# Norms of keys and queries from matmuls with ones, one chain of roots per head, and ScalarE Sqrt in the last stage

## The chip, the cores and the metric

The kernel runs on one core of a Trainium2 chip. The metric is the device time of one execution in microseconds (us); the times shown are medians of several executions. The engines are named as in the profile: PE (TensorE, matmuls), PEld (its weight loads), DVE (VectorE), ACT (ScalarE), POOL (GpSimd) and SP (SyncE, which issues nearly all the DMAs here).

## The reference

One layer of a hybrid encoder on a sequence of 2048 tokens and 1024 channels. Cut to what matters:

```python
h = rms_norm(x, norm_w) * (1.0 + scale) + shift          # scale, shift, gate from c
proj = h @ w_in                                          # u_a, z_a, qkv, z_b, beta, alpha
y = s5_direction(u, ..., False) + s5_direction(u, ..., True) + s5_d * u
y_a = glu(gelu(y)) * jax.nn.silu(z_a)                    # branch A: state space

qkv = jax.nn.silu(centred_depthwise_conv(qkv, conv_w))   # 5 taps, per channel
q = l2_normalize(to_heads(q)) * (DN_HEAD_DIM ** -0.5)    # 4 heads of 128
k = l2_normalize(to_heads(k))
o = gated_delta_chunked(q, k, v, g_f, beta_f) + flip(gated_delta_chunked(flip(q), ...))
o = o * lax.rsqrt(jnp.mean(o * o, axis=-1) + NORM_EPS) * dn_norm_w
y_b = o * jax.nn.silu(z_b)                               # branch B: gated delta rule

x = x + gate * (jnp.concatenate([y_a, y_b]) @ w_out)
out = rms_norm(x, final_norm_w)

def l2_normalize(t):
    return t * lax.rsqrt(jnp.sum(t * t, axis=-1, keepdims=True) + NORM_EPS)
```

The two places that the change touches are `l2_normalize` of K and Q, and the two root-mean-square norms at the end, that of `o` (128 channels of a head) and that of the output row (1024 channels).

## The kernel before

The stages follow each other: the modulation and `h` with the first columns of the projection (to about 195 us), the projection with the convolutions of K, Q and V beside the preparation of the state-space branch (to about 800), the inverses of the delta rule's chunks, and from about 1200 us the last stage, in which the scan over chunks, the output projection and the final norm run together.

**Ticks.** The projection works in ticks. `job(i, evac)` takes one block of 128 columns of `w_in`; for each of its four blocks of 512 tokens, `gemm` runs 24 matmuls of 128x512 (three products of 16-bit halves, tiles `hhi`, `hlo`, `wh`, `wl`) into a PSUM bank of the pool `gm`, `evac` takes the bank out, and `tick()` runs what is due. `later(n, fn)` puts `fn` n ticks on. The order in which the functions are called is the order on each engine's queue. The columns come in the order: u, part of z_a, beta and alpha, four heads of K, four of Q, then V in turn with the rest of z_a and z_b. Each head's block takes its steps one tick apart: `tap` (ACT, first tap, L1014), `conv` (DVE, four operations on 128x512, L1021), `gated` (ACT Silu, L1027), `turn` (PE, four transposes to PSUM, L1037; ACT, four Squares with a sum each, L1046), `norm` (DVE: for K the root `rk` and the product `kt`, L1056, L113 to L120, L1059; for Q only `iq2`, L1053), and for K `back` (PE, four transposes of `kt`, L1066; ACT copy, L1068).

`rsqrt` is a chain of 11 DVE operations: two on integers for a first guess (L113, L115) and three rounds of three (L118 to L120).

**The state-space branch** runs as a generator, `side`, of which `tick` takes one step. In its tables, `s5_tables`, POOL forms 12 products of 128x512 per group (`cpw`, `bpw`, `tmp`, helper line L502), PE transposes `bpw` into the pool `sq`, ACT copies it to `bpt` (L832, one buffer for two copies per group) and SP stores it to `cb_d`; other matmuls give `lk`, which ACT copies (L852) and POOL adds to.

**PSUM.** The pools are `gm` with 2 banks, `pt` with 3 and `sq` with 2. Transposes of K, Q and V, the column maxima (`w_max`: a matmul of `w` with `ones` for the scale of the next weights, DVE L135 to L139) and later stages share `pt`. The next weights' low half is `wl` (DVE, L215).

**The last stage** follows order strings written by hand, one letter for each step of a generator:

```python
S9 = "qqqqsssssssqsssqlttltststqstrrsrrtssssssltrltrr"
in_order(order, s=seq(s), l=ahead_of(s + 1), a=part(ag, NA[s]),
         p=product(prev) if prev is not None else iter(()), q=prepare(s - 1), r=product(s - 1),
         t=prepare(NCH - s))
```

`seq(s)` is a step of the scan (tiles `z`, `vn`, `S`, `tq`), `prepare(ch)` norms a chunk of `o` (`rs`, then POOL's `on`, L1718, PE's transposes, L1722, DVE's `yb`, L1724, ACT's `oyh`), and `product(ch)` makes 128 rows of the output (`r`, norm `r1`, store). There are 16 of each.

Of the kernel before, what the change touches and what calls it, by code (L numbers as in the profile page):

```python
# [40 lines left out]
def block(ctx, tc, x, c, ada_w, ada_b, norm_w, w_in, conv_w,  # L41
# [66 lines left out]
    def rsqrt(pool, dst, src, tag):  # L108

        shp = list(src.shape)  # L110
        y = pool.tile(shp, F32, tag=tag + "y", name=tag + "y")
# [1 line left out]
        V.tensor_scalar(out=t.bitcast(I32), in0=src.bitcast(I32), scalar1=1, scalar2=None,  # L113
                        op0=ALU.arith_shift_right)
        V.tensor_scalar(out=y.bitcast(I32), in0=t.bitcast(I32), scalar1=-1.0,  # L115
                        scalar2=float(0x5F3759DF), op0=ALU.mult, op1=ALU.add)
        for it in range(3):
            V.tensor_tensor(out=t, in0=y, in1=y, op=ALU.mult)  # L118
# [1 line left out]
            V.scalar_tensor_tensor(out=(dst if it == 2 else y), in0=t, scalar=1.5, in1=y,  # L120
                                   op0=ALU.add, op1=ALU.mult)
# [678 lines left out]
    def s5_tables(gb, st5, sc_, bt):  # L800
# [26 lines left out]
        for i in range(2):  # L827
            ps = bank("sq", (128, GB, 128))
            for j in range(GB):
                nc.tensor.transpose(ps[:, j], bpw[i][:, j].rearrange("p t q -> p (t q)"), ident)  # L830
# [1 line left out]
            A.activation(out=bpt, in_=ps, func=AF.Copy)  # L832
# [19 lines left out]
        A.activation(out=l0, in_=lk[0][:, 0:SN], func=AF.Copy)  # L852
# [145 lines left out]
    def conv_job(i, kind, h):  # L998
# [26 lines left out]
        def gated(tb):  # L1025
            cv = cvs[tb]
            A.activation(out=cv, in_=cv, func=AF.Silu)  # L1027
# [4 lines left out]
        def turn(tb):
# [5 lines left out]
            if kind == 2:  # L1038
# [3 lines left out]
                return  # L1042
            ss = sp.tile([128, 4], F32, tag="ss", name="ss")
            for j in range(4):
                jk = sp.tile([128, 128], BF16, tag="jk", name="jk")
                A.activation(out=jk, in_=ps[:, j * 128:(j + 1) * 128], func=AF.Square,  # L1046
                             accum_out=ss[:, j:j + 1])
# [2 lines left out]
        def norm(ps, ss, c4):  # L1050
            if kind == 0:

                V.tensor_scalar(out=iq2[:, c4, h], in0=ss, scalar1=EPS, scalar2=128.0, op0=ALU.add, op1=ALU.mult)  # L1053
                return
            rk = sp.tile([128, 4], F32, tag="rk", name="rk")
            V.tensor_scalar(out=ss, in0=ss, scalar1=EPS, scalar2=None, op0=ALU.add)  # L1056
            rsqrt(sp, rk, ss, "rk")
            kt = tp.tile([128, 4, 128], F32, tag="kt", name="kt")
            V.tensor_tensor(out=kt, in0=ps.rearrange("p (c d) -> p c d", d=128), in1=bc(rk, 128), op=ALU.mult)  # L1059
# [636 lines left out]
    def prepare(ch):  # L1696
# [16 lines left out]
        V.scalar_tensor_tensor(out=sq, in0=sq, scalar=1.0 / 128, in1=t, op0=ALU.mult, op1=ALU.add)  # L1713
# [4 lines left out]
        P.tensor_tensor(out=on, in0=o_, in1=bc(rs, 128), op=ALU.mult)  # L1718
# [15 lines left out]
    def product(ch):  # L1734
        yh, yl, xt = bs_.pop(ch)
        r = ot.tile([128, D], F32, tag="r", name="r", bufs=2)
        s2 = ot.tile([128, 2], F32, tag="s2", name="s2", bufs=2)
# [9 lines left out]
        jk = ot.tile([128, D], BF16, tag="jkr", name="jkr")  # L1747
        for n in range(2):
            ns = slice(n * 512, (n + 1) * 512)
            A.activation(out=jk[:, ns], in_=r[:, ns], func=AF.Square, accum_out=s2[:, n:n + 1])  # L1750
# [2 lines left out]
        V.tensor_tensor(out=s1, in0=s2[:, 0:1], in1=s2[:, 1:2], op=ALU.add)
# [4 lines left out]
        V.scalar_tensor_tensor(out=r, in0=r, scalar=r1, in1=fnw, op0=ALU.mult, op1=ALU.mult)
# [80 lines left out]
```

## Time and profile before

| what | value |
|---|---|
| median of 3 runs | 1452.25 us (1451.58 to 1455.87) |
| profiled execution | 1450.6 us |
| its span, first to last instruction | 1448.9 us |
| mean granted clock of PE | 0.947 |
| busy: PE, DVE, ACT, POOL | 1288.1, 1143.8, 683.0, 728.6 us |
| DMA, mean over the span | 142 GB/s |

The shares are averages over stages with different limits. Where two engines are both busy for most of a stage, the windows of the profile tell which of them waits. The granted clock is that of the windows' own rows: 1.00 is full speed.

### The profile page before, as it was taken

To read this page: it belongs to the slowest core of one execution; us is meant where nothing else is said; L and a number is where in the kernel's file an instruction comes from. 1 tells how busy PE (TensorE), PEld (TensorE's weight loads), DVE (VectorE), ACT (ScalarE), POOL (GpSimd) and SP (SyncE) were. 2 spreads that over 40 slices of the span, in tenths; PEclk is the share of its full clock that TensorE was granted. 3 is DMA by queue.
4 is the path that set the end of the run, shared out by engine and by line. 5 is a ranking of instruction groups with operands and counts; after the bars stand their busy time and mean duration, and the time that the engine had idled before them with its cause. 6 is when DMAs were issued, how large, how long until landed. Compare 5 with 4: busy or idle time off the path is not lost.

```text
span 1448.9 us, 26795 instructions
## 1 busy us (share of the span) xinstructions
PE 1288.1 (89%) x9744; PEld 890.1 (61%) x9744; DVE 1143.8 (79%) x2483; ACT 683.0 (47%) x1571; POOL 728.6 (50%) x680
## 2 busy tenths in 40 slices
PE   2879897888879988999999799999999988899996
PEld 2435343444444444555455578999998776788884
DVE  4645588999988899999984667888887467998875
ACT  4445222445546545353446566777666322323322
POOL 3223123763553377878760666556652234554443
PEclk9889998988989999999999899999999999899998
DMA  9454433224326533443424523544435487486532
GB/s 314 152 132 138 104 68 93 62 70 142 105 88 166 155 98 99 132 123 96 139 76 147 156 72 110 169 140 140 125 118 191 152 298 271 165 300 209 189 118 79
DMA packets 255284, 206.46 MB, mean 142 GB/s; under 512 B 88496, under 2 KB 206256, under 8 KB 255152
## 3 DMA queue, kind: packets, MB, share of 16 engines
q1 hardware_dynamic: 255152, 204.75, 45.6%
q8 instruction: 77, 1.26, 0.4%
q14 instruction: 55, 0.45, 0.1%
HBM read 133.38 MB, written 73.33 MB: 143 GB/s over the span
## 4 chain that ended last, share of the span: by engine, by line
PE 50%; DVE 32%; DMA 5%; issue 4%; POOL 3%; ACT 2%; SPq 1%; POOLq 0%; DVEq 0%; ACTq 0%
PE gm L33 27%; PE sq L33 13%; PE pt L33 8%; DVE cv L1021 6%; DVE w L502 3%; DVE xs L930 2%; DVE rkt L119 1%; DVE wl L215 1%; DVE rkt L118 1%; DMA y<-ya_d 1%; DVE tm L502 1%; DVE r L1744 1%; DMA cb_d<-bpt 1%; DVE rky L120 1%; PE pt L1037 1%
## 5 line engine op out<-in xcount | busy, mean ns | idle before, releaser
L33 PE MATMUL gm<-hhi,wh 128*128 128x512 f16 (+1 forms) x784 | 297.5, 396 | 13.0 <-ACT wh L213 6.9
L33 PE MATMUL gm<-hhi,wl 128*128 128x512 f16 (+1 forms) x784 | 295.5, 392 | 13.4 <-DVE wl L215 13.4
L33 PE MATMUL gm<-hlo,wh 128*128 128x512 f16 (+1 forms) x784 | 296.5, 394 | 0.0
L33 PEld LDWEIGHTS <-wh 128*128 128x128 f16 (+1 forms) x1664 | 154.3, 100 | 202.7 <-issue 31.2
L1021 DVE SCALAR_TENSOR_TENSOR cv<-raw,cw,cv 128x512 f32<-128x512 f32 x192 | 185.7, 970 | 9.2 <-ACT cv L1014 3.2
L33 PEld LDWEIGHTS <-wl 128*128 128x128 f16 (+1 forms) x832 | 80.2, 100 | 114.6 <-DVE wl L215 18.0
L502 POOL TENSOR_TENSOR w<-w,w 128x512 f32<-128x512 f32 x32 | 50.1, 1574 | 73.3 <-DVE w L502 73.3
L33 PE MATMUL gm<-yh,gwh 128*128 128x256 f32 x256 | 80.0, 313 | 6.3 <-ACT yh L770 5.3
L1006 ACT ACTIVATE raw<-gm,w 128x512 f32<-128x512 f32 x48 | 33.1, 690 | 110.4 <-PE gm L33 110.4
L1745 POOL TENSOR_TENSOR r<-r,xt 128x512 f32<-128x512 f32 x32 | 45.7, 1429 | 69.0 <-DVE r L1744 33.7
L33 PE MATMUL gm<-yl,gwh 128*128 128x256 f32 x256 | 73.4, 287 | 0.7 <-POOL yl L771 0.7
L33 PE MATMUL gm<-yh,gwl 128*128 128x256 f32 x256 | 72.5, 283 | 0.0
L1413 ACT ACTIVATE Y<-pt 128x512 f16<-128x512 f32 x96 | 57.9, 603 | 25.6 <-PE pt L33 24.8
L33 PE MATMUL sq<-S,kq 128*128 128x128 f32 x480 | 65.4, 291 | 0.0
L930 DVE TENSOR_TENSOR_SCAN xs<-c,w 128x255 f32<-128x255 f32 x64 | 63.5, 1050 | 2.2 <-POOL w L502 2.2
L33 PEld LDWEIGHTS sq<-S,kq 128*128 128x128 f32 x480 | 63.0, 205 | 2.0
L1392 DVE CAST_PREDICATED pb<-msk,pt 128x512 f16<-128x512 int8 x80 | 56.7, 711 | 6.5 <-PE pt L33 5.3
L33 PE MATMUL pt<-Y,nh 128*128 128x64 f16 (+1 forms) x896 | 56.3, 198 | 4.6 <-DVE Y L1400 4.2
L312 POOL TENSOR_SCALAR hhi<-hf 128x512 f16<-128x512 f32 x32 | 30.0, 957 | 54.7 <-ACT hf L310 47.4
L1414 ACT ACTIVATE YT<-pt 128x512 f16<-128x512 f32 x96 | 57.3, 597 | 0.0
L994 ACT ACTIVATE z<-gm,w 128x512 f32<-128x512 f32 x32 | 22.0, 687 | 74.1 <-PE gm L33 43.2
L1665 POOL TENSOR_TENSOR ra<-ra,xh 128x512 f32<-128x512 f32 x14 | 18.8, 1346 | 75.4 <-DVE ra L1664 44.7
(455 smaller groups left out, 3627.7 us busy)
## 6 DMA issues: line engine op xcount, KB each, us to landing
xt<-in_x_dram SPq DMA_DIRECT2D x25, 512.0 KB
ws<-in_w_in_dram SPq DMA_DIRECT2D x24, 512.0 KB
aw<-in_ada_w_dram SPq DMA_DIRECT2D x24, 512.0 KB
kq<-kT_d SPq DMA_DIRECT2D x32, 256.0 KB
kq<-qT_d SPq DMA_DIRECT2D x32, 256.0 KB
kt<-kt_d SPq DMA_DIRECT2D x32, 256.0 KB
vt<-vt_d SPq DMA_DIRECT2D x32, 256.0 KB
out_dram<-r SPq DMA_DIRECT2D x16, 512.0 KB
```

Of the source, the lines that this page charges most:

```text
L33: nc.tensor.matmul(out, lhsT, rhs, start=start, stop=stop)
L312: P.tensor_scalar(out=hhi[:, k, sl], in0=hf, scalar1=1.0, scalar2=1.0, op0=ALU.mult, op1=ALU.mult)
L502: (e or V).tensor_tensor(out=o, in0=a, in1=b, op=op)
L930: V.tensor_tensor_scan(out=o, data0=m1, data1=v, initial=0.0, op0=ALU.mult, op1=ALU.add)
L994: A.activation(out=z, in_=ps, func=AF.Silu, scale=iv)
L1006: A.activation(out=raw[:, 2 + tb * 512:2 + (tb + 1) * 512], in_=ps, func=AF.Copy, scale=iv)
L1021: V.scalar_tensor_tensor(out=cv, in0=raw[:, o + j:o + j + 512], scalar=cw[:, i12, j:j + 1], in1=cv, op0=ALU.mult, op1=ALU.add)
L1392: V.copy_predicated(out=cols(PB[d][li], b, d), mask=mb, data=pp.rearrange("p t (n b) -> p t n b", b=b))
L1413: A.activation(out=cols(Y[d], b, d), in_=pa.rearrange("p t (n b) -> p t n b", b=b), func=AF.Copy)
L1414: A.activation(out=cols(YT[d], b, 1 - d), in_=pb.rearrange("p t (n b) -> p t n b", b=b), func=AF.Copy)
L1665: P.tensor_tensor(out=r_, in0=r_, in1=x_, op=ALU.add)
L1745: P.tensor_tensor(out=r[:, ns], in0=r[:, ns], in1=xt[:, ns], op=ALU.add)
```

## The change

1. **K and Q.** ACT squares the convolved block in one operation of 128x512 (`sq`, before the transposes), and `total` sums it over channels with four PE matmuls against a column of ones into a `pt` bank. `taken` (DVE) brings the four columns to SBUF: into `ss` for K, into `iq2` for Q. Q isn't transposed any more. K has one `rsqrt` for a head, on 16 columns, after its fourth block; then its four blocks are transposed, one a tick. Functions that are due in the same tick are sorted by a rank.
2. **Tables.** `bpt` has a buffer for each of its two copies, and a `yield` stands between ACT's copies of `lk` and POOL's additions and the store of `lk_d`. Some buffers move: `raw` has two instead of three, `cv` nine instead of five, `kt` three instead of two; `qh` shares the buffer of `q`; scratch of the beta and alpha columns shares that of `sq`.
3. **Last stage.** The root is ACT Sqrt followed, after a `yield`, by `root_fix` on DVE: a reciprocal and one round of three operations. In `product`, one Square over 1024 replaces two over 512 and the addition of their sums; in `prepare`, an operation with `iq2` goes, since `iq2` now holds the factor.

```diff
+    def root_fix(pool, y, src, tag):
+        t = pool.tile(list(src.shape), F32, tag=tag + "t", name=tag + "t")
+        V.reciprocal(out=y, in_=y)
+        V.tensor_tensor(out=t, in0=y, in1=y, op=ALU.mult)
+        V.scalar_tensor_tensor(out=t, in0=t, scalar=-0.5, in1=src, op0=ALU.mult, op1=ALU.mult)
+        V.scalar_tensor_tensor(out=y, in0=t, scalar=1.5, in1=y, op0=ALU.add, op1=ALU.mult)
...
-    rp = p1.enter_context(pool("rp", 3))
+    rp = p1.enter_context(pool("rp", 2))
...
-            bpt = bt.tile([128, GB, 128], F32, tag="bpt", name="bpt")
+            bpt = sc_.tile([128, GB, 128], F32, tag=f"tp{1 + i}", name="bpt", bufs=1)
...
         A.activation(out=lkf[:, W:], in_=lk[0][:, SN:W], func=AF.Copy)
+        yield
         TT(l0, l0, dd[:, gb], ALU.add, P)
...
-        q = mp.tile([128, 2, R // 2], F32, tag="qh", name="qh", bufs=1)
+        q = mp.tile([128, 2, R], F32, tag="q", name="qh", bufs=1)[:, :, 0:R // 2]
...
-        for e in [e for e in late if e[0] <= clock[0]]:
+        for e in sorted((e for e in late if e[0] <= clock[0]), key=lambda e: e[2]):
...
-            later(1, lambda: turn(tb))
+            if kind == 2:
+                later(1, lambda: turn(tb))
+                return
+            sq = tp.tile([128, 512], F32, tag="sq", name="sq")
+            A.activation(out=sq, in_=cv, func=AF.Square)
+            later(1, lambda: total(tb, sq), 2)
+
+        def total(tb, sq):
+            ps = bank("pt")
+            for j in range(4):
+                mm(nc, ps[:, j:j + 1], sq[:, j * 128:(j + 1) * 128], ones[:, 0:1])
+            later(1, lambda: taken(tb, ps), 1)
+
+        def taken(tb, ps):
+            c4 = slice(tb * 4, tb * 4 + 4)
+            if kind == 0:
+                V.tensor_scalar(out=iq2[:, c4, h], in0=ps[:, 0:4], scalar1=EPS, scalar2=128.0 * EPS,
+                                op0=ALU.add, op1=ALU.mult)
+                cvs.pop(tb)
+                return
+            V.tensor_scalar(out=ss[:, c4], in0=ps[:, 0:4], scalar1=EPS, scalar2=None, op0=ALU.add)
+            if tb == NB - 1:
+                rsqrt(sp, rk, ss, "rk")
+                for n in range(NB):
+                    later(1 + n, lambda n=n: turn(n), 2)
...
-            ss = sp.tile([128, 4], F32, tag="ss", name="ss")
-            for j in range(4):
-                jk = sp.tile([128, 128], BF16, tag="jk", name="jk")
-                A.activation(out=jk, in_=ps[:, j * 128:(j + 1) * 128], func=AF.Square,
-                             accum_out=ss[:, j:j + 1])
-            later(1, lambda: norm(ps, ss, c4))
...
+            later(1, lambda: norm(ps, c4), 1)
...
-            later(2, lambda: back(kt, c4))
+            later(2, lambda: back(kt, c4), 1.5)
...
-        t = ot.tile([128, H], F32, tag="sqt", name="sqt")
-        V.tensor_scalar(out=t, in0=iq2[:, ch, :], scalar1=EPS, scalar2=None, op0=ALU.mult)
-        V.scalar_tensor_tensor(out=sq, in0=sq, scalar=1.0 / 128, in1=t, op0=ALU.mult, op1=ALU.add)
+        V.scalar_tensor_tensor(out=sq, in0=sq, scalar=1.0 / 128, in1=iq2[:, ch, :], op0=ALU.mult, op1=ALU.add)
         rs = ot.tile([128, H], F32, tag="rs", name="rs")
-        rsqrt(ot, rs, sq, "ro")
-        yield
+        A.activation(out=rs, in_=sq, func=AF.Sqrt)
+        yield
+        root_fix(ot, rs, sq, "ro")
...
-        for n in range(2):
-            ns = slice(n * 512, (n + 1) * 512)
-            A.activation(out=jk[:, ns], in_=r[:, ns], func=AF.Square, accum_out=s2[:, n:n + 1])
-        yield
-        V.tensor_tensor(out=s1, in0=s2[:, 0:1], in1=s2[:, 1:2], op=ALU.add)
+        A.activation(out=jk, in_=r, func=AF.Square, accum_out=s1)
+        yield
         V.tensor_scalar(out=s1, in0=s1, scalar1=1.0 / D, scalar2=EPS, op0=ALU.mult, op1=ALU.add)
-        rsqrt(ot, r1, s1, "rf")
-        yield
+        A.activation(out=r1, in_=s1, func=AF.Sqrt)
+        yield
+        root_fix(ot, r1, s1, "rf")
```

**Where the instructions stand.** PE in the projection, at the end of a tick in which a K block is turned and another turned back (`gm` are the last matmuls of the tick, `sq<-ident,bpw` the tables' transposes); before:

```order
L33 MATMUL gm<-hhi,wl 128x512
L1066 MATMUL pt<-ident,kt 128x128 x4
L1037 MATMUL pt<-ident,cv 128x128 x4
L830 MATMUL sq<-ident,bpw_2882 128x128 x4
L830 MATMUL sq<-ident,bpw_2883 128x128 x4
L33 LDWEIGHTS wh
```

and a tick of the same kind after:

```order
L33 MATMUL gm<-hhi,wl 128x512
L1092 MATMUL pt<-ident,kt 128x128 x4
L1075 MATMUL pt<-ident,cv 128x128 x4
L33 MATMUL pt<-ones,sq 128x1 x4
L838 MATMUL sq<-ident,bpw_3568 128x128 x4
L838 MATMUL sq<-ident,bpw_3569 128x128 x4
L33 LDWEIGHTS wh
```

A third group stands on the `pt` banks in one tick, the sums of a later block.

DVE in the same part of the program (`cv` are the convolution's steps, `kt` the normed K); before, with a chain for each block:

```order
L1021 SCALAR_TENSOR_TENSOR cv<-raw,cw,cv 128x512 x8
L1056 TENSOR_SCALAR ss<-ss 128x4
L113 TENSOR_SCALAR rkt<-ss 128x4
L115 TENSOR_SCALAR rky<-rkt 128x4
L118 TENSOR_TENSOR rkt<-rky 128x4
L119 SCALAR_TENSOR_TENSOR rkt<-rkt,ss 128x4
L120 SCALAR_TENSOR_TENSOR rky<-rkt,rky 128x4
L118 TENSOR_TENSOR rkt<-rky 128x4
```

and after, between two of the chains:

```order
L1032 SCALAR_TENSOR_TENSOR cv<-raw,cw,cv 128x512 x4
L1063 TENSOR_SCALAR kss<-pt 128x4
L1085 TENSOR_TENSOR kt<-pt,rk 128x512
L223 SCALAR_TENSOR_TENSOR wl<-ws,w_3686,wh 128x1024
L1032 SCALAR_TENSOR_TENSOR cv<-raw,cw,cv 128x512 x4
L1085 TENSOR_TENSOR kt<-pt,rk 128x512
L1063 TENSOR_SCALAR kss<-pt 128x4
```

The chain is gone from between the convolution and `kt`; `kss`, which reads a `pt` bank, and `kt` follow the convolution.

ACT near the end of the last stage (`jk` and `jkr` are the Squares, `oyh` the copy of `yb`); before:

```order
L1709 ACTIVATE jk,sq<-o 128x128 x4
L1640 ACTIVATE ayh<-y_17088 128x512
L1709 ACTIVATE jk,sq<-o 128x128 x4
L1750 ACTIVATE jkr,s_17034<-r 128x512 x2
L1727 ACTIVATE oyh<-yb 128x512 x2
```

and after, with the roots `rs` and `r_16602`:

```order
L1736 ACTIVATE jk,sq<-o 128x128 x4
L1740 ACTIVATE rs<-sq 128x4
L1774 ACTIVATE jkr,s_16601<-r 128x1024
L1753 ACTIVATE oyh<-yb 128x512
L1777 ACTIVATE r_16602<-s_16601 128x1
L1753 ACTIVATE oyh<-yb 128x512
```

The two kinds of root are new on this engine, the first right behind its Squares, the second here behind a copy that waits for DVE's `yb`. In all the program has 33 ACT table loads, where it had 32.

More of the change, by code (lines that the diff above doesn't have):

```diff
@@ L962, in block, with later @@
     clock = [0]
-    def later(n, fn):
-        late.append((clock[0] + n, fn))
+    def later(n, fn, rank=0):
+        late.append((clock[0] + n, fn, rank))
     def tick():
         clock[0] += 1
-        for e in [e for e in late if e[0] <= clock[0]]:
+        for e in sorted((e for e in late if e[0] <= clock[0]), key=lambda e: e[2]):
             late.remove(e)
@@ L1003, in conv_job @@
         cvs = {}
+        if kind == 1:
+            ss, rk = [sp.tile([128, NCH], F32, tag=t, name=t, bufs=2) for t in ("kss", "rk")]
         def evac(tb, ps, iv):
@@ L1012, in tap @@
         def tap(tb):
-            cv = cvs[tb] = tp.tile([128, 512], F32, tag="cv", name="cv", bufs=5)
+            cv = cvs[tb] = tp.tile([128, 512], F32, tag="cv", name="cv", bufs=9)
             A.activation(out=cv, in_=raw[:, tb * 512:tb * 512 + 512], func=AF.Copy, scale=cw[:, i12, 0:1])
@@ L1042, in turn, with norm @@
                 return
-            ss = sp.tile([128, 4], F32, tag="ss", name="ss")
-            for j in range(4):
-                jk = sp.tile([128, 128], BF16, tag="jk", name="jk")
-                A.activation(out=jk, in_=ps[:, j * 128:(j + 1) * 128], func=AF.Square,
-                             accum_out=ss[:, j:j + 1])
-            later(1, lambda: norm(ps, ss, c4))
[L1050 to L1059, printed above, removed]
+            later(1, lambda: norm(ps, c4), 1)
+        def norm(ps, c4):
+            kt = tp.tile([128, 4, 128], F32, tag="kt", name="kt", bufs=3)
+            V.tensor_tensor(out=kt, in0=ps.rearrange("p (c d) -> p c d", d=128), in1=bc(rk[:, c4], 128), op=ALU.mult)
             nc.sync.dma_start(out=kt_d[:, c4, h, :], in_=kt)
-            later(2, lambda: back(kt, c4))
+            later(2, lambda: back(kt, c4), 1.5)
         def back(kt, c4):
@@ L1113, in ab_parts @@
     def ab_parts(av):
-        t = lambda n: tp.tile([128, 2, NCH, H], F32, tag=n, name=n, bufs=1)
         al = av[1]
-        ab_, e, s, s2, w_ = t("abs"), t("e"), t("s"), t("s2"), t("w_")
+        room = [tp.tile([128, 4, 2, NCH, H], F32, tag="sq", name="room") for _ in range(2)]
+        ab_, e, s, s2, w_ = [room[n // 4][:, n % 4] for n in range(5)]
         dnr = tp.tile([128, 4, H], F32, tag="dnr", name="dnr", bufs=1)
@@ L1736, in product @@
         r = ot.tile([128, D], F32, tag="r", name="r", bufs=2)
-        s2 = ot.tile([128, 2], F32, tag="s2", name="s2", bufs=2)
         for n in range(2):
@@ L1747, in product @@
         jk = ot.tile([128, D], BF16, tag="jkr", name="jkr")
-        for n in range(2):
-            ns = slice(n * 512, (n + 1) * 512)
-            A.activation(out=jk[:, ns], in_=r[:, ns], func=AF.Square, accum_out=s2[:, n:n + 1])
+        s1, r1 = [ot.tile([128, 1], F32, tag=t, name=t, bufs=2) for t in ("s1", "r1")]
+        A.activation(out=jk, in_=r, func=AF.Square, accum_out=s1)
         yield
-        s1 = ot.tile([128, 1], F32, tag="s1", name="s1", bufs=2)
-        V.tensor_tensor(out=s1, in0=s2[:, 0:1], in1=s2[:, 1:2], op=ALU.add)
         V.tensor_scalar(out=s1, in0=s1, scalar1=1.0 / D, scalar2=EPS, op0=ALU.mult, op1=ALU.add)
-        r1 = ot.tile([128, 1], F32, tag="r1", name="r1", bufs=2)
-        rsqrt(ot, r1, s1, "rf")
+        A.activation(out=r1, in_=s1, func=AF.Sqrt)
         yield
+        root_fix(ot, r1, s1, "rf")
         V.scalar_tensor_tensor(out=r, in0=r, scalar=r1, in1=fnw, op0=ALU.mult, op1=ALU.mult)
```

## The prediction

> **What bounds the kernel now.** I read the page's busy shares first, then the busy time by stage, then the chain and the groups by line in the two stages that the diff touches, and the timeline where one piece had to be priced.
>
> ```profile
> PE 1288.1 (89%) x9744; PEld 890.1 (61%) x9744; DVE 1143.8 (79%) x2483; ACT 683.0 (47%) x1571; POOL 728.6 (50%) x680
> ```
>
> PE is the fullest engine, but that is an average. The blocks of K and Q go through the convolution from about 252 to 506 us. The next view splits most of that time (window, length, busy us of PE, PEld, DVE, ACT and POOL, granted clock, DMA share, GB/s):
>
> ```profile
> 260.00:300.00 40.00, 34.40 (x224) 16.86 (x221) 38.85 (x59) 15.81 (x45) 33.06 (x26) 0.96 0.23 73
> 300.00:340.00 40.00, 32.68 (x184) 17.23 (x184) 37.48 (x85) 20.29 (x68) 19.98 (x20) 0.87 0.34 99
> 340.00:380.00 40.00, 29.40 (x163) 14.19 (x161) 37.92 (x66) 16.64 (x60) 24.45 (x23) 0.86 0.30 89
> 380.00:420.00 40.00, 30.22 (x196) 16.63 (x197) 35.92 (x91) 18.09 (x61) 16.33 (x15) 0.80 0.43 129
> 420.00:440.00 20.00, 19.71 (x137) 10.88 (x136) 17.39 (x38) 9.94 (x34) 7.60 (x8) 1.00 0.29 86
> 440.00:480.00 40.00, 38.39 (x197) 19.81 (x196) 32.66 (x59) 27.51 (x97) 12.21 (x14) 1.00 0.68 175
> sum 220.00, PE 184.81 PEld 95.59 DVE 200.22 ACT 108.27 POOL 113.63; mean PE 30.80 PEld 15.93 DVE 33.37 ACT 18.05 POOL 18.94
> ```
>
> From 260 to 420 DVE is busy for 90 to 97% of the time while PE waits. PE is idle for 220 - 184.81 = 35.2 us, and it is also slowed: busy time times (1 - clock) is 1.4 + 4.2 + 4.1 + 6.0 = 15.7 us. So there are 51 us of room here, nearly all before 440; after it PE is full. What holds DVE is one chain of roots after another. This is the timeline of one (start, duration), DVE's and then POOL's rows of the same moment:
>
> ```profile
> 311.69 0.98 DVE L113 TENSOR_SCALAR rkt<-ss 128x4 int32<-128x4 int32 x1
> 312.70 0.17 DVE L115 TENSOR_SCALAR rky<-rkt 128x4 int32<-128x4 int32 x1
> 312.90 1.11 DVE L118 TENSOR_TENSOR rkt<-rky 128x4 f32<-128x4 f32 x1
> ...
> 319.64 1.11 DVE L120 SCALAR_TENSOR_TENSOR rk<-rkt,rky 128x4 f32<-128x4 f32 x1
> ```
>
> ```profile
> 311.59 1.05 POOL L502 TENSOR_TENSOR tmp<-pwci,cr 128x512 f32<-128x512 f32 x1
> 312.72 1.27 POOL L502 TENSOR_TENSOR cpw<-cpw,tmp 128x512 f32<-128x512 f32 x1
> ```
>
> Eleven operations on 4 numbers per partition take 9.1 us (311.69 to 320.75), because each wide product on POOL holds up the small DVE operation beside it: 0.98 to 1.11 us instead of 0.17.
>
> The last stage, 1200 to 1449, is another case:
>
> ```profile
> 1200.00:1300.00 100.00, 85.41 (x503) 74.46 (x502) 86.63 (x262) 33.17 (x125) 53.08 (x43) 0.93 0.68 238
> 1300.00:1400.00 100.00, 97.46 (x545) 82.58 (x544) 81.46 (x264) 31.18 (x110) 47.44 (x38) 1.00 0.56 192
> ```
>
> PE has 14.6 us of idle time and 85.41 x 0.07 = 6.0 us of lost clock in the first 100 us, and next to nothing in the second.
>
> **The change, part by part: K and Q.** Their costs, by line from 195 to 800 us (the first row is all DVE work that touches the chains' scratch tile, 16 chains of 11; the last two are the wait lines of ACT and PE):
>
> ```profile
> 195.00:800.00 605.00, 61.39 (x176) 0.94 0.37 109
> L1056 DVE TENSOR_SCALAR ss<-ss 128x4 f32<-128x4 f32 x16 | 5.4, 337 | 0.8 <-ACT jk L1046 0.8
> L1046 ACT ACTIVATE jk<-pt 128x128 bf16<-128x128 f32 x128 | 33.6, 287 | 2.8 <-PE pt L1037 2.8
> L1046 ACT ACTIVATION_READ_ACCUMULATOR jk<-pt 128x1 f32 x128 | 28.0, 220 | 0.0
> L1027 ACT ACTIVATE cv<-cv 128x512 f32<-128x512 f32 x48 | 30.7, 640 | 1.2 <-DVE cv L1021 1.2
> ACT bpt L832 <- DMA cb_d<-bpt: 62.5, 8, 14.7
> PE gm L33 <- DVE wl L215: 13.4, 5, 5.6
> ```
>
> - DVE: a chain costs 61.39/16 = 3.84 us. Four stay of 16, now on 16 columns, which I price alike since the row is time of issue and waiting: -46 us. The 32 `taken` of 0.34 us (row L1056) make 11 us, against 5.4 of `ss` and about as much of Q's, so they cancel. DVE's 200.2 us in the window become about 154.
> - ACT: 128 Squares with their reads go, 61.6 us; 32 Squares of 128x512 come, at the Silu's 0.64 us 20.5. ACT gains 41 us and was not the bound.
> - PE pays. The timeline prices four matmuls with `ones` and four transposes:
>
> ```profile
> 63.63 0.36 PE L33 MATMUL pt<-ones,aw 128*128 128x1 f32 x2
> 63.85 0.36 PE L33 MATMUL pt<-ones,acc 128*128 128x1 f32 x2
> 306.25 0.60 PE L1066 MATMUL pt<-ident,kt 128*128 128x128 f32 x4
> 306.69 0.60 PE L1037 MATMUL pt<-ident,cv 128*128 128x128 f32 x4
> ```
>
>   Starts lie 0.22 us apart, so a block's four sums take 0.9 us and its four transposes 0.44. K keeps its transposes: 16 x 0.9 = 14.3 us. Q loses them: 16 x 0.46 = 7.3. PE gets 21.6 us more, of which 19.8 fall in the window.
> - The room in the window becomes 51 - 20 = 31 us. Not all is had. The next column block's weights (`wl`, 13.4 us of PE's waits) come behind DVE's queue: with DVE a quarter shorter I take half, -6.7. Second, in 13 ticks `back`, `turn` and `total` now use all three `pt` banks, where a K tick used two; PE then waits in the same tick for DVE's `taken` and `norm`, which stand behind four convolution steps. No row shows this wait. The nearest is the idle time ahead of the same transposes, in the last row below: 11.9 us over 48 blocks, 0.25 us each. I take that in each of 32 ticks, since `taken` is new in all, -8.0. Bounds: none, and 1.5 us a tick, the one piece in the row before it, which ended on neither a root nor a `bpt` copy.
> - `bpt`, with two buffers: ACT's 62.5 us of waiting for a store goes. What of it reached PE is in the room already, so nothing is added. The `yield` lets POOL compute the next products instead of waiting for ACT's copies; POOL's 12 products stay, `lk_d` is stored a tick later, behind one tick's other transfers on SP, which issues as many as before. `qh` in `q`'s buffer: both are POOL's, in order. `raw` with two buffers instead of three: a head's last convolution comes three ticks after its last block, and the buffer is wanted again after four, a tick of slack. These I count as nothing; if the cover goes, SP's `kt_d` store, which waits for `kt`, holds `cb_d` behind it, as in the 4.23 us piece of the chain.
>
> ```profile
> 381.27 4.23 DMA cb_d<-bpt
> 444.42 0.66 PE L1037 MATMUL pt<-ident,cv 128*128 128x128 f32 x4 [1.50 <-ACT cv L1027]
> L1037 PE MATMUL pt<-ident,cv 128*128 128x128 f32 x192 | 30.8, 285 | 11.9 <-ACT kk L1068 5.7 <-DVE kt L1059 4.2 <-ACT cv L1027 1.5
> ```
>
> Sum for this stage: 31 - 6.7 - 8.0 - 1.8 (Q's additions after 480) = **14.5 us less**. Bounds: 31 less, and 25 more where the new wait is 1.5 us a tick (32 x 1.5 = 48, against 31 - 6.7 - 1.8 = 22.5 of room).
>
> The row says 46 us less on DVE. A rule would give less: the Trainium skill, "SBUF — State Buffer", section "SBUF: two separate sides", says that DVE (with two SBUF inputs or in a fast mode) and GpSimd take turns on a shared port pair, each for a whole instruction. Then POOL's products only move on to hold up the convolutions, and a chain is worth its own time, 11 x 0.17 = 1.9 us: 12 chains are 22 us. The alternation above agrees; with 22 the stage could gain no more than about that, with 46 up to the 31.
>
> **The last stage.** Rows from 1200 on (first all DVE work on the scratch tile of `rs`, then that of `r1`; 16 chains each), and two prices for ACT from elsewhere:
>
> ```profile
> 1200.00:1449.00 249.00, 39.22 (x176) 0.96 0.54 188
> 1200.00:1449.00 249.00, 35.60 (x176) 0.96 0.54 188
> L1713 DVE SCALAR_TENSOR_TENSOR sq<-sq,sqt 128x4 f32<-128x4 f32 x16 | 9.2, 575 | 2.4 <-ACT jk L1709 1.0
> L118 DVE TENSOR_TENSOR rot<-roy 128x4 f32<-128x4 f32 x48 | 11.0, 229 | 1.6
> L1722 PE MATMUL sq<-ident,on 128*128 128x128 f32 x64 | 11.1, 301 | 14.6 <-POOL on L1718 14.6
> L852 ACT ACTIVATE l<-sq 128x16 f32<-128x16 f32 x8 | 1.8, 219 | 0.0
> L954 ACT ACT_TABLE_LOAD x13 | 16.7, 1283 | 0.2
> ACT oyh L1727 <- DVE yb L1724: 40.4, 9, 8.2
> ```
>
> - Removed: 39.2 + 35.6 us of chains. Added: 32 x 4 operations at L118's 0.229, 29 us (the reciprocal too, which no row shows on so few numbers). DVE gets 46 us back in a stage where it was busy for four fifths. ACT adds 32 Sqrts at 0.22 (7 us) and one more table load in the program, 1.3 us.
> - PE's waits here are for `on`, 14.6 us, and POOL's `on` waits for `rs`. The root was 39.2/16 = 2.5 us; it becomes 0.22 + 4 x 0.23 = 1.1 and two handoffs. But `root_fix` now stands a step later, and the Sqrt stands in ACT's queue, behind copies that wait for others (`oyh`: 40.4/9 = 4.5 us a time). I take half of waits and lost clock, (14.6 + 6.0)/2 = 10.3. Bounds: all of it, -21; three Sqrts behind a waiting `oyh`, +13.
> - The end, where nothing covers:
>
> ```profile
> 1441.31 0.16 DVE L1753 TENSOR_TENSOR s<-s 128x1 f32<-128x1 f32 x1 [1.90 <-ACT jkr L1750]
> 1443.89 1.28 DVE L1758 SCALAR_TENSOR_TENSOR r<-r,r,fnw 128x1024 f32<-128x1024 f32 x1
> ```
>
>   From 1441.31 to 1443.89 are 2.6 us. They become a step of 0.2, a Sqrt of 0.22, four steps of 0.2 and two handoffs of about 0.1: 1.4. The Square over 1024 instead of the second 512 adds some 0.5 (three quarters of the Silu's 0.64): -0.7.
>
> Sum: **11 us less**. Together 1450.6 - 14.5 - 11 = 1425.1 for a profiled execution. The one before stands 1.65 under the median of 1452.25, so 1427.
>
> **Rivals.**
> A. *The PE work and the third bank eat the convolution stage's gain.* Were the new wait 0.7 us a tick instead of 0.25 (32 x 0.7 = 22.5), nothing is left there: 1452 - 11 = 1441. For it: `taken` stands behind four convolution steps. Against it: the steps begin at the tick's start, and 24 matmuls hide them.
> B. *Slower.* The same wait, larger: at 1.05 us a tick the stage has lost the last stage's 11 as well (32 x 1.05 = 33.5) and the sign turns; at the bound of 1.5 it is 25 - 11 more: 1466. For it: POOL's products can hold up each of the four steps ahead. Against it: a wait of that length stands once in the 48 blocks, and only 13 of the 32 ticks need all three banks.
> C. *Full gain.* Both stages reach their bounds, 31 and 21 less: 1400. Half the weights' waits and all waits for `on` would have to go, and DVE and POOL hold each other up still; half way there is 1413.
> D. *The Sqrt reloads tables.* Were a load put ahead of each of 32 Sqrts and one behind it, each root would come 2 x 1.283 = 2.6 us later, less the 1.4 (2.5 - 1.1) that it gains: 16 x 1.2 = 19 us more ahead of `on`, and 1452 - 14.5 + 19 = 1457. The built program has one load more, not 64. The Trainium skill, "ScalarE: Activation LUTs", section "Table sets: the hidden batching unit", has sqrt in a set of its own and tells to batch by set; only Copy and Square stand beside Sqrt here, and no run yet shows them together.
>
> **How the numbers follow.** Forecast 1427 (1416 to 1437): 0.58. A: 0.18. C: 0.13. B: 0.06. D: 0.02. Nothing measurable: 0.03, from between A and B. What lies within 0.3% (4.4 us) can't be told from no change here. A counts as faster but for 0.02: faster 0.87, same 0.05, slower 0.08. The range 1407 to 1446 takes in the forecast, A, and C to half way, and leaves out B, D and the rest of C.
>
> **What would show it.** Right: in the K ticks DVE well under 90%, granted clock over 0.95 from 300 to 420, PE idle from 260 to 480 down from 35 to about 15; no wait of ACT for `cb_d`; PE's wait for `on` about halved and one more table load. Wrong: PE's waits for `taken` or `norm` at `total` and `turn` beyond 0.7 us a tick, or ACT's Sqrt held up behind `oyh` with `on` later than before.

## The result, and the profile after

The changed kernel takes 1428.3 us (median of 4 runs, 1426.4 to 1430.0) against 1454.1 before: a ratio of 0.9829, with a 95% interval of 0.9813 to 0.9845. The forecast was 1427. The sum came out, but not term by term: tried by itself, the convolution stage gave less than forecast and the last stage more. (The pool `sq` has three PSUM banks, not the two that the part on the kernel gives; no step above used that number.)

The profiled execution has a span of 1427.1 us at a mean clock of 0.952. The busy shares of its page:

```profile
PE 1297.3 (91%) x9936; PEld 907.2 (64%) x9936; DVE 1057.0 (74%) x2095; ACT 672.9 (47%) x1348; POOL 733.2 (51%) x680
```

The windows of the convolution stage, as they were shown of before:

```profile
260.00:300.00 40.00, 33.87 (x225) 17.32 (x223) 35.78 (x86) 17.24 (x43) 25.03 (x23) 0.91 0.24 73
300.00:340.00 40.00, 33.99 (x210) 19.53 (x209) 33.38 (x45) 17.25 (x38) 25.62 (x23) 0.91 0.19 53
340.00:380.00 40.00, 36.67 (x250) 21.20 (x249) 34.44 (x45) 18.21 (x36) 28.32 (x23) 0.91 0.39 116
380.00:420.00 40.00, 36.81 (x230) 21.88 (x229) 28.23 (x49) 19.37 (x43) 23.75 (x20) 0.91 0.33 96
420.00:440.00 20.00, 20.00 (x144) 11.68 (x143) 13.97 (x31) 9.21 (x19) 9.20 (x14) 1.00 0.72 196
440.00:480.00 40.00, 39.87 (x228) 23.05 (x227) 24.23 (x49) 21.63 (x37) 0.98 (x1) 1.00 0.83 214
sum 220.00, PE 201.21 PEld 114.67 DVE 170.04 ACT 102.91 POOL 112.90; mean PE 33.54 PEld 19.11 DVE 28.34 ACT 17.15 POOL 18.82
```

PE's idle time fell from 35.2 to 18.8 us, but the clock did not recover: 0.91 in four windows, 12.7 us lost where 15.7 were. Two thirds of what PE still waits for is the release of a PSUM bank, and it waited for such banks before, too. These are the longest of PE's waits from 260 to 480 (total, times, longest) in the kernel before:

```profile
PE gm L33 <- DVE wl L215: 10.5, 3, 5.6
PE pt L1066 <- DVE w L135: 5.9, 1, 5.9
PE pt L1037 <- ACT kk L1068: 5.7, 3, 4.3
PE pt L33 <- DVE kt L1059: 4.6, 1, 4.6
PE pt L1037 <- DVE kt L1059: 4.2, 2, 3.9
```

`kk`, `kt` and `w` are what empties the `pt` banks, so some 21 us of PE's waits were for these banks already. After the change the whole list is this, 12.5 us for `pt`; below it stands the longest wait in the timeline, DVE's rows first:

```profile
PE pt L1075 <- DVE kss L1063: 6.4, 2, 6.0
PE gm L33 <- DVE wl L223: 6.1, 1, 6.1
PE pt L33 <- DVE raw L1011: 3.0, 1, 3.0
PE pt L1075 <- DVE kt L1085: 1.9, 1, 1.9
PE pt L1092 <- DVE kt L1085: 1.2, 1, 1.2
```

```profile
326.75 0.24 DVE L120 SCALAR_TENSOR_TENSOR rk<-rkt,rky 128x16 f32<-128x16 f32 x1
326.91 3.10 DVE L1032 SCALAR_TENSOR_TENSOR cv<-raw,cw,cv 128x512 f32<-128x512 f32 x4
329.93 0.15 DVE L1063 TENSOR_SCALAR kss<-pt 128x4 f32<-128x4 f32 x1
...
330.14 1.11 PE L1075 MATMUL pt<-ident,cv 128*128 128x128 f32 x4 [6.01 <-DVE kss L1063]
```

DVE has a chain of roots and then four convolution steps ahead of a `kss` of 0.15 us, and until `kss` has read its bank PE can't turn the next block.

In the last stage, 100-us windows 25 us earlier than those shown of before (the first `on` comes 7.5 us earlier and the last `r` 20.3, so the places match only roughly; in a window from 1192.5, where the shift of the first `on` would put it, PE is busy for 95.0 us instead of 94.4):

```profile
1175.00:1275.00 100.00, 94.44 (x591) 82.40 (x591) 70.01 (x180) 37.07 (x130) 59.90 (x49) 0.98 0.81 281
1275.00:1375.00 100.00, 93.13 (x520) 80.49 (x519) 59.67 (x154) 31.67 (x112) 44.03 (x36) 0.97 0.57 198
```

The first gained 9 us of PE time and most of its clock; DVE fell from 87% to 70%. The second lost 4 us: it has 6.9 us of idle time, all of it one wait for `on`, which the timeline explains (engines mixed, in order of time):

```profile
1310.29 0.63 ACT L1667 ACTIVATE ayh<-y 128x512 fp32r<-128x512 f32 x1 [8.18 <-DMA y<-ya_d]
1310.95 0.69 DVE L1671 TENSOR_TENSOR ayl<-y,ayh 128x512 fp32r<-128x512 f32 x1 [5.30 <-ACT ayh L1667]
1311.56 0.17 DVE L126 RECIPROCAL rs<-rs 128x4 f32<-128x4 f32 x1
...
1312.16 0.16 DVE L129 SCALAR_TENSOR_TENSOR rs<-rot,rs 128x4 f32<-128x4 f32 x1
1312.49 1.04 POOL L1744 TENSOR_TENSOR on<-o,rs 128x512 f32<-128x512 f32 x1 [8.45 <-DMA of<-o_d]
1313.58 1.12 PE L1748 MATMUL sq<-ident,on 128*128 128x128 f32 x4 [6.87 <-POOL on L1744]
```

ACT's `ayh` waits for the load of `y`, DVE's `ayl` waits for `ayh`, and `root_fix` stands behind `ayl`. POOL's wait is put down to the load of `of`, but POOL starts 0.17 us after `rs` is done (1312.16 + 0.16), so I read `rs` as what let it go.

### The profile page after: what moved, and what is told of

It reads as the page before. It is cut to its first block, busy times and chain, and to the rows that moved or that the text cites. A ratio compares the mean times of both kernels' runs of the same rounds, so it can differ in the third digit from the quotient of the medians.

```text
span 1427.1 us, 26499 instructions
## 1 busy us (share of the span) xinstructions
PE 1297.3 (91%) x9936; PEld 907.2 (64%) x9936; DVE 1057.0 (74%) x2095; ACT 672.9 (47%) x1348; POOL 733.2 (51%) x680
## 3 DMA queue, kind: packets, MB, share of 16 engines
q8 instruction: 78, 1.28, 0.4%
## 4 chain that ended last, share of the span: by engine, by line
PE 64%; DVE 21%; DMA 4%; issue 3%; ACT 3%; POOL 1%; SPq 1%; DVEq 0%; ACTq 0%; POOLq 0%
PE gm L33 36%; PE sq L33 15%; PE pt L33 12%; DVE cv L1032 6%; DVE w L510 2%; DMA y<-ya_d 1%; DVE xs L939 1%; DVE tm L510 1%; DVE wl L223 1%; PE pt L1075 1%; DVE t L510 1%; DMA kq<-qT_d 1%; DVE YT L1432 1%; DVE pb L1419 1%; PE sq L1748 1%
## 5 line engine op out<-in xcount | busy, mean ns | idle before, releaser
L1032 DVE SCALAR_TENSOR_TENSOR cv<-raw,cw,cv 128x512 f32<-128x512 f32 x192 | 197.5, 1030 | 31.4 <-ACT cv L1025 26.3
L1770 POOL TENSOR_TENSOR r<-r,xt 128x512 f32<-128x512 f32 x32 | 41.5, 1297 | 62.2 <-DVE r L1769 29.1
L1440 ACT ACTIVATE Y<-pt 128x512 f16<-128x512 f32 x96 | 58.0, 604 | 24.5 <-PE pt L33 22.9
L33 PE MATMUL sq<-S,kq 128*128 128x128 f32 x480 | 62.4, 282 | 0.0
L33 PEld LDWEIGHTS sq<-S,kq 128*128 128x128 f32 x480 | 60.0, 196 | 2.0
L33 PEld LDWEIGHTS <-nh 128*128 128x128 f16 x1024 | 48.2, 98 | 13.7 <-issue 6.6
L223 DVE SCALAR_TENSOR_TENSOR wl<-ws,w,wh 128x1024 f16<-128x1024 f32 (+1 forms) x25 | 36.2, 1448 | 27.6 <-ACT wh L221 27.6
```

Source lines behind the costliest of these rows:

```text
L33: nc.tensor.matmul(out, lhsT, rhs, start=start, stop=stop)
L223: V.scalar_tensor_tensor(out=wl, in0=ws, scalar=s, in1=wh, op0=ALU.mult, op1=ALU.subtract)
L1032: V.scalar_tensor_tensor(out=cv, in0=raw[:, o + j:o + j + 512], scalar=cw[:, i12, j:j + 1], in1=cv, op0=ALU.mult, op1=ALU.add)
L1440: A.activation(out=cols(Y[d], b, d), in_=pa.rearrange("p t (n b) -> p t n b", b=b), func=AF.Copy)
L1770: P.tensor_tensor(out=r[:, ns], in0=r[:, ns], in1=xt[:, ns], op=ALU.add)
```

## The experiments

Two theories stood at the start. One: the two stages are independent; the last one gave some 14 to 18 us, and the convolution stage little, since PE's new work and the waits for a bank took what DVE gave. The other: the tables' buffers did much of it, or the last stage gained by its new start. Of each kernel the table gives how many us earlier (minus) than before an event came in its profile; the first column of numbers is the time before. The events are the first, 16th, 32nd and last copy `raw<-gm`, POOL's first `on`, and its last `r<-r,xt`.

| event | before | change | e1 | e4 | e5 | e6 | e9 | e11 | e12 |
|---|---|---|---|---|---|---|---|---|---|
| K begins | 256.8 | +1.7 | +0.4 | +2.4 | +5.2 | +0.2 | +2.8 | +1.5 | +2.4 |
| K done | 390.3 | -8.4 | -14.2 | -18.7 | -1.9 | -23.8 | -21.5 | -8.5 | -7.6 |
| Q done | 505.6 | -2.2 | -3.1 | -9.3 | +10.0 | -16.2 | -14.1 | -13.3 | -2.9 |
| V done | 750.6 | -3.7 | -7.8 | -12.4 | +3.1 | -21.7 | -17.2 | -16.5 | -7.2 |
| first `on` | 1204.7 | -7.5 | -9.3 | -8.6 | +3.4 | -20.2 | -15.6 | -13.3 | -6.9 |
| last `r` | 1438.3 | -20.3 | -9.4 | -22.9 | -9.8 | -34.9 | -36.6 | -27.0 | -11.4 |

Between V's end and the first `on` these kernels have the same code but for the first root, yet the difference moves there by -3.8 to +3.8 us. So a single profile places a gain to within some 4 us; the medians decide. Read with that margin, the second column says where the change gained: K's blocks came through 10.1 us faster (+1.7 to -8.4), and Q's gave 6.2 of it back (-8.4 to -2.2).

**e1_norms: the norms of K and Q alone.** `bpt` and the additions as before, last stage as before:

```diff
-            bpt = sc_.tile([128, GB, 128], F32, tag=f"tp{1 + i}", name="bpt", bufs=1)
+            bpt = bt.tile([128, GB, 128], F32, tag="bpt", name="bpt")
...
-        yield                                    # ahead of TT(l0, l0, dd[:, gb], ALU.add, P)
...
+        rsqrt(ot, rs, sq, "ro")                  # prepare and product of before
```

> The norms of K and Q as changed (sums by matmuls with ones, one chain of roots a head, the buffers that go with it); one bpt buffer, no extra yield and the last stage as before. Theory: the convolution stage gained only about 4 us (the last evacuation of raw came 3.7 us earlier in the changed kernel), because PE's 20 us of new work and the waits for a third pt bank, 12.5 us in five pieces, each with half clock behind it, took DVE's gain; so 0 to 6 us under before, 1448 to 1454. Rival: the gain there came from the two bpt buffers, without which ACT's waits for the store come back on PE's path: no faster than before, and ACT waits for cb_d by over 40 us.

Measured 1446.1, ratio 0.9927 (0.9904 to 0.9951): 7 to 14 us faster, somewhat more than the 0 to 6 expected and clearly not the rival. ACT waits for the one `bpt` buffer 21.3 us, where it was 62.5 (total, times, longest):

```profile
ACT bpt L840 <- DMA cb_d<-bpt: 21.3, 8, 3.0
```

**e2_tables: the tables' part alone.** The two edits above, put into the kernel before.

> Only the tables' part: two bpt buffers and the yield ahead of POOL's additions; norms and last stage as before. Theory: what ACT waits for the store lies beside PE's wait for DVE's roots, so within 0.3% of before (1450 to 1458), though ACT's wait for cb_d is gone. Rival: the store was on the path (three pieces of 3 to 4 us in the chain between 380 and 440), 5 to 11 us under before.

Measured 1454.3, ratio 0.9997 (0.9985 to 1.0009). ACT's 62.5 us of waits for the store are gone from its list, and the time is the same: by the interval no more than some 2 us of it was on PE's path.

**e3_last: the last stage alone.** `root_fix`, `prepare` and `product` of the change in the kernel before, with `scalar2=128.0 * EPS` in `norm`.

> Only the last stage as changed (ACT Sqrt and root_fix, one Square over 1024); norms and tables as before. Theory: the last stage is independent of what comes ahead and gave 14 to 18 of the 25.7 us: 1436 to 1441. Rival: part of it came from the stage's start (loads and PSUM in another phase after a shorter projection), so only 8 to 11 us alone: 1443 to 1447.

Measured 1440.4, ratio 0.9895 (0.9873 to 0.9916): 12 to 18 us, the theory's. The three parts alone give 8.6, 0.3 and 14.2, together 23.1 of the 25.7 us, so they add up within their intervals.

**e4_first: the bank released ahead of the convolution.**

```diff
-            later(1, lambda: taken(tb, ps), 1)
+            later(1, lambda: taken(tb, ps), -1)
...
-                rsqrt(sp, rk, ss, "rk")
+                later(1, lambda: rsqrt(sp, rk, ss, "rk"), 0.5)
...
-            later(1, lambda: norm(ps, c4), 1)
+            later(1, lambda: norm(ps, c4), -1)
```

> The changed kernel with taken and norm sorted ahead of the convolution of the same tick, and the chain of roots a tick later, behind the convolution. Theory: PE's waits at turn and total come from DVE's four convolution steps ahead of the release of the bank; so the 12.5 us of waits for kss, kt and raw go and half of the clock loss of 12.7 us with them: 10 to 18 us under the changed kernel, 1410 to 1419. Rival: DVE and POOL together are the bound there, and the waits only move to the evacuation or to wl: within 0.3% of the changed kernel, 1424 to 1433.

Measured 1425.0, ratio 0.9789 (0.9772 to 0.9806), 3.4 us under the changed kernel: far less than expected, and inside the rival's range, though not by its mechanism. The waits for `kt` are gone, and neither the evacuation nor `wl` took their place, but another bank's wait did, that for the bank of the weights' column maximum, which DVE takes out (L143) between two convolutions (PE's waits from 260 to 480; the rest of the list is 0.5 us for `kss`):

```profile
PE pt L33 <- DVE w L143: 8.7, 3, 3.7
PE gm L33 <- DVE wl L223: 6.5, 1, 6.5
```

In such a tick four users want three banks.

**e5_sqbank: the sums in a bank of `sq`.**

```diff
         def total(tb, sq):
-            ps = bank("pt")
+            ps = bank("sq")
```

> The changed kernel with the sums of total in a bank of the pool sq, which the tables hardly use there, so that pt serves two users a tick as before. Theory: the third user of pt is what PE waits for; the 12.5 us of waits for kss, kt and raw at turn and total go but for single pieces under 1 us, and with them about half of the 13.6 us of half clock from 280 to 510: 8 to 15 us under the changed kernel, 1413 to 1420. Rival: DVE is late with kt in any case (turn's bank is released by kt behind the convolution), so the waits stay at turn and back: under 4 us.

Measured 1436.9, ratio 0.9886 (0.9863 to 0.9909): 8.5 us slower than the changed kernel. The theory as I had put it falls: it isn't the number of users of `pt` alone. The waits moved with the bank. In the timeline the state-space branch's matmul, which needs `sq`, now waits for DVE's late read of Q's sums, which stands behind four convolution steps (3.10 us from 503.45):

```profile
506.47 0.16 DVE L1059 TENSOR_SCALAR iq<-sq 128x4 f32<-128x4 f32 x1
...
506.68 1.98 PE L33 MATMUL sq<-uT,bpt 128*64 128x256 f32 x8 [5.47 <-DVE iq L1059]
```

About 3.5 us of the loss stand ahead of K (the first row of the table), where this edit changes no instruction; the profile doesn't say why.

**e6_both: e4 and e5 together.**

> As the last one, and taken and norm sorted ahead of the convolution, the chain of roots a tick later. Theory: what e4_first left (9.2 us, for the bank of the column maximum) and what stays with sq's bank (kt behind the convolution) go both: 10 to 18 us under the changed kernel, 1410 to 1418, and at most the 6 us wait for wl at 283 us stays of PE's waits there. Rival: PE is full in the Q ticks and takes back what K's gain: as e4_first, 1422 to 1427.

Measured 1414.0, ratio 0.9733 (0.9716 to 0.9750): 14.3 us under the changed kernel, as the theory had it. Neither the early release nor the other pool was enough here by itself. The list of PE's waits from 260 to 510 begins so (1.5 us for `kss` and `kt` follow), and below it is the sum of the windows from 260 to 480:

```profile
PE gm L33 <- DVE wl L223: 6.5, 1, 6.5
PE sq L33 <- DVE iq L1059: 4.7, 2, 2.5
PE pt L1092 <- DVE w L143: 2.1, 1, 2.1
```

```profile
sum 220.00, PE 208.66 PEld 120.31 DVE 190.04 ACT 108.70 POOL 126.78; mean PE 34.78 PEld 20.05 DVE 31.67 ACT 18.12 POOL 21.13
```

PE is idle for 11.3 us there and, with a clock of 0.91 and 0.96 in two of the windows, loses some 4.5 to the clock: 15.8 us of room, where the changed kernel has 18.8 + 12.7 = 31.5. Of the 12.5 us of waits for the `pt` banks and the sums, 3.6 are left in these windows.

**e7_near: `root_fix` of `rs` ahead of its `yield`.**

```diff
         A.activation(out=rs, in_=sq, func=AF.Sqrt)
+        root_fix(ot, rs, sq, "ro")
         yield
-        root_fix(ot, rs, sq, "ro")
```

> The changed kernel with root_fix of rs ahead of the yield, right behind its Sqrt on DVE's queue. Theory: PE's longest wait of the last stage (6.87 us at 1313 for on) comes from root_fix standing behind ayl, which waits over ACT's ayh for the load of y; with root_fix ahead of it that wait goes: 4 to 8 us under the changed kernel, 1420 to 1424. Rival: the load of y holds PE's own matmuls at the same moment anyway, and DVE now waits for ACT 16 times: no faster, 1427 to 1433.

Measured 1422.3, ratio 0.9806 (0.9772 to 0.9839), 6.0 us under the changed kernel in the medians, as the theory had it; the intervals of the two ratios overlap. The trace shows the mechanism: the wait at 1313 is gone and PE doesn't idle in the second 100 us.

```profile
1275.00:1375.00 100.00, 100.00 (x569) 86.28 (x567) 66.19 (x162) 34.00 (x119) 45.83 (x38) 1.00 0.59 203
```

**e8_rounds: three rounds in `root_fix`**, ten operations of DVE instead of four:

```diff
         V.reciprocal(out=y, in_=y)
-        V.tensor_tensor(out=t, in0=y, in1=y, op=ALU.mult)
+        for it in range(3):
+            V.tensor_tensor(out=t, in0=y, in1=y, op=ALU.mult)
...
```

> The changed kernel with three rounds in root_fix, 10 operations of DVE instead of 4, so that DVE has nearly the old chain's 11 and ACT the Sqrt. Theory: the last stage gained by DVE's time (192 operations come back, at 0.23 us 44 us of DVE): 8 to 14 us over the changed kernel, 1436 to 1442. Rival: it gained by the merged Squares, the dropped operations and the shorter way to on alone, and DVE has room there (60 to 70% busy): under 4 us, 1428 to 1432.

Measured 1453.8, ratio 1.0002 (0.9983 to 1.0020): 25.5 us over the changed kernel, more than either theory, and all that the change had gained. The 192 operations cost 0.13 us each on the whole, in a stage where DVE isn't full. From the first `on` to the end, and the group of PE's transposes of `on`, first of the changed kernel:

```profile
1197.00:1426.00 229.00, 210.39 (x1184) 180.37 (x1184) 143.76 (x352) 74.72 (x259) 113.98 (x93) 0.96 0.57 199
```

```profile
L1748 PE MATMUL sq<-ident,on 128*128 128x128 f32 x64 | 10.7, 293 | 10.6 <-POOL on L1744 10.6
```

and of this one:

```profile
1198.00:1450.00 252.00, 217.49 (x1184) 184.06 (x1184) 178.98 (x544) 75.05 (x259) 111.27 (x93) 0.94 0.52 181
```

```profile
L1749 PE MATMUL sq<-ident,on 128*128 128x128 f32 x64 | 11.5, 308 | 21.4 <-POOL on L1745 21.4
```

DVE is busy for 63% and 71% of these. PE runs the same 1184 matmuls, the waits for `on` double (10.8 us more), and PE is busy for 7.1 us longer at a lower clock. Two things are in this price and the run doesn't part them: what stands behind the added operations in DVE's queue, and the root of `rs` itself, which now comes later for `on`.

**e9_three: e4, K's sums in `sq` and Q's in `pt`, and e7.**

```diff
-            ps = bank("pt")
+            ps = bank("sq" if kind == 1 else "pt")       # with the edits of e4 and e7
```

> The changed kernel with three edits: taken and norm ahead of the convolution with the chain a tick later, K's sums in a bank of sq (Q's stay in pt), and root_fix of rs ahead of its yield. Theory: they act at different places (e6_both 14.3 us, e7_near 6.0), and add up: 18 to 22 us under the changed kernel, 1406 to 1410. Rival: the last stage starts earlier and runs into the load of y or the clock in another way, so only e6's part stays: 1412 to 1416.

Measured 1412.5, ratio 0.9728 (0.9696 to 0.9760), the lowest median of all, though not apart from e6. The rival's range holds. By the table it is not the last stage that failed to add: from the first `on` to the last `r` e9 gained 21.0 us against e6's 14.7. But it was 4.6 us behind e6 at the first `on`, 2.6 of them as K began, ahead of all edits. So the rival's time came, and not by its mechanism; whether e6 with e7 alone would be lower was not tried.

**e10_near2: also `root_fix` of `r1` ahead of its `yield`.**

> As the last one, and root_fix of r1 ahead of its yield too. Theory: r1 releases only the store of the output rows, off PE's path, and DVE now waits for ACT 16 times more: 0 to 4 us slower than the last one. Rival: it frees ACT and r's buffers earlier: 2 to 5 us faster.

Measured 1414.0, ratio 0.9729 (0.9708 to 0.9750): within what these runs can tell of e9. Neither side is shown.

**e11_no_q: Q's Squares and sums left out**, `iq2` set to one by a `memset`, so that q isn't normed.

> The changed kernel without the Squares and sums of Q: iq2 is set to one, so q isn't normed. Theory: PE is full in Q's ticks, so the 16 x 0.9 us of its sums come off the time whole, with the waits for iq: 12 to 18 us under the changed kernel, 1410 to 1416. Rival: the ticks wait for DVE or ACT there and the sums are hidden: under 5 us.

Measured 1422.2, ratio 0.9797 (0.9770 to 0.9824): 6.1 us under the changed kernel in the medians, between the two; the intervals of the two ratios overlap. In the profile Q is done 11.1 us earlier than in the changed kernel, near the 14.3 at which the prediction priced 16 sums; by the first `on` 5.8 are left. Where the rest went in unchanged code stays open.

**e12_rs_only: the old chain of 11 for `r1`.**

```diff
-        A.activation(out=r1, in_=s1, func=AF.Sqrt)
-        yield
-        root_fix(ot, r1, s1, "rf")
+        rsqrt(ot, r1, s1, "rf")
+        yield
```

> The changed kernel with the old chain of 11 for r1, while rs keeps Sqrt and root_fix. Theory: the last stage gains where on waits for rs, and r1 holds up nothing but the store: within 5 us of the changed kernel, 1426 to 1433. Rival: the chain stands in DVE's queue ahead of the scan's and of on's steps, and its 112 operations more cost half of what three rounds in both roots cost: 10 to 14 us, 1438 to 1442.

Measured 1438.9, ratio 0.9912 (0.9883 to 0.9941): 10.6 us over the changed kernel, the rival's range. That is 112 operations at 0.095 us each, with 16 Sqrts fewer on ACT. Until the last rows `r1` releases only the store, so I read the price as that of standing in DVE's queue ahead of the steps that PE does need. The profile bears this out in part: 1.7 of the 10.6 us come after the last `r`, where nothing covers the chain; from the first `on` on PE's listed waits are 15.0 us instead of 11.5 (for `on` 12.8 instead of 10.6), and its 1184 matmuls are busy for 214.3 us instead of 210.4 at a lower clock. No single wait shows the queue at work.

## Why the prediction was right, point by point

**The sum.** Forecast 14.5 + 11 = 25.5 us, measured 25.7; but e1 gives 8.6 (7 to 14) for the norms and e3 14.2 (12 to 18) for the last stage. One term was too large and one too small, and they cancelled: that the number came out this close is luck. Of the signs that the prediction named, ACT's wait for `cb_d` is gone, DVE is at 71 to 89% from 260 to 420 and one table load was added; the clock from 300 to 420 is 0.91 and not over 0.95, PE's idle time is 18.8 and not about 15, and the waits for `on` were not halved.

**DVE's 46 us in the convolution stage.** The chains fell as forecast: all DVE work on their scratch tile is now

```profile
195.00:780.00 585.00, 18.17 (x44) 0.95 0.38 111
```

and these groups stand beside it:

```profile
L1032 DVE SCALAR_TENSOR_TENSOR cv<-raw,cw,cv 128x512 f32<-128x512 f32 x192 | 197.5, 1030 | 31.4 <-ACT cv L1025 26.3
L1063 DVE TENSOR_SCALAR kss<-pt 128x4 f32<-128x4 f32 x16 | 2.4, 151 | 0.0
L33 PE MATMUL pt<-ones,sq 128*128 128x1 f32 x256 | 31.9, 246 | 5.5 <-DVE raw L1011 3.0 <-DVE iq L1059 2.4
```

61.4 - 18.2 = 43 us less, and four chains on 16 columns at 4.5 us each against 3.84 on four. But DVE's busy time from 260 to 480 fell by 30 only: the convolution's steps, the same 192, rose from 185.7 to 197.5 us. A step takes 0.75 us where POOL is idle and 1.27 on the mean where POOL works beside it, and 102 steps now stand beside POOL's work where 89 did. So POOL's products hold up what is left on DVE instead. This agrees with the rule of the Trainium skill ("SBUF — State Buffer", "SBUF: two separate sides") that DVE and POOL take turns on a shared port pair. By the rule the prediction had 22, by the row 46; 30 lies between. `taken` costs 0.15 us, not 0.34: it reads PSUM and no row of it shows a hold-up.

**PE's 21.6 us.** Right in size: the sums are busy for 31.9 us (row above), and the transposes of `turn` fell from 30.8 us (192 of them) to 20.6 (128), 21.7 us more in all. e11 shows that in Q's ticks most of their price is paid: 11.1 us by Q's end, though only 6.1 are left in the time.

**The waits for the third bank, 8.0 us, and the clock.** This is the step that was mis-sized. The wait is there and its cause was the one named, `taken` and `norm` behind four convolution steps: 12.5 us from 260 to 480. But they come as five waits of 0.4 to 6 us and not as 0.25 a tick, and I had let all the lost clock go, while 12.7 us of it stayed. I had also taken the 0.25 from one line (L1037) and overlooked that before the change PE waited some 21 us for `pt` banks: these waits fell from some 21 us to 12.5, where I had only added 8.0 for a new user, and the column maxima were a user of these banks that I didn't count. Remaining room was 31.5 us, where I had left 14.7. e6 shows the size of it: with most of these waits gone the room is 15.8 us and the kernel 14.3 us faster.

**The weights' wait**, taken at half of 13.4: over the whole run 9.2 stayed, and in the window, where it had been 10.5, 6.1 in one piece. **`bpt` at nothing**: right, by e2.

**The last stage.** Forecast 10.3 + 0.7. The gain came, but not as forecast: the waits for `on` were to be halved and went from 14.6 to 10.6, 6.87 of them in the one wait that the forecast had named as its risk, `root_fix` a step later. What I undersized is DVE's queue. I had counted 46 us of DVE as room in a stage where it wasn't full, and priced only the way to `on`. By e12 and e8 each small operation costs 0.10 to 0.13 us of the end time there; for `r1` I put that down to its place in the queue, for `rs` the later root is in it too. In number the roots lost 32 x 7 = 224 operations: at that rate 21 to 30 us. e3's 14.2 are less, so by this estimate the Sqrt on ACT and the later `root_fix` gave some 7 or more back. This split was not tried by itself, but e8 bears on it: with ten operations instead of eleven its last stage was 8.2 us longer than before's (+2.2 at the last `r`, -6.0 at the first `on`).

**The end.** From the merged Square's sum to the scaling of the last rows:

```profile
1420.79 0.15 DVE L1776 TENSOR_SCALAR s<-s 128x1 f32<-128x1 f32 x1
1420.97 0.20 ACT L1777 ACTIVATE r<-s 128x1 f32<-128x1 f32 x1 [0.52 <-DVE s L1776]
1422.07 1.28 DVE L1780 SCALAR_TENSOR_TENSOR r<-r,r,fnw 128x1024 f32<-128x1024 f32 x1
```

1.28 us, forecast 1.4; the Square takes 1.06 instead of 0.63.

**The rivals.** A (the bank eats the stage's gain) came true in part: the measured wait lies between the forecast's and A's. B's price of 1.05 us a tick was not reached: the 12.5 us are 0.39 in each of the 32 ticks. C did not come either, not even half way to 1413; e6 comes near that time, but by edits that the change doesn't have. D did not happen: one table load, and a Sqrt of 0.21 us.

```profile
L1740 ACT ACT_TABLE_LOAD x1 | 1.3, 1283 | 0.0
L1740 ACT ACTIVATE rs<-sq 128x4 f32<-128x4 f32 x16 | 3.3, 207 | 12.6 <-DVE sq L1738 12.6
```

## What to carry to other kernels

When an engine's queue is in order, place what releases a shared bank first in its step, and count who else wants that bank in the same step; e4 and e5 alone gave 3.4 us less and 8.5 us more, both together 14.3 less. The price of small operations is not read from an engine's busy share but from what stands behind them or waits for them: 192 of them cost 25.5 us on an engine that was 63% busy. When a sum of terms comes out, test the terms; here one was too large and one too small.
